# Moving the operand tile of the half-width products within SBUF, and leaving out their one split product

## The chip, the cores and the metric

The kernel runs on one core of a Trainium2 chip. The metric is the device time of one execution in microseconds; several executions are taken, and their median counts. Lower is better.

## The reference

One encoder layer over 512 positions of width 1024, everything in float32:

```python
x = x + 0.5 * swiglu(rms_norm(x, ffn1_norm), ffn1_w_gate, ffn1_w_up, ffn1_w_down)
h = rms_norm(x, mix_norm)
u = h @ w_in                      # [ fourier group 512 | q 8x64 | k 2x64 | v 2x64 ]
f_out = fourier_mixer(u[..., :o0], fnet_w, fnet_b)
a_out = gqa_attention(u[..., o0:o1], u[..., o1:o2], u[..., o2:], q_norm, k_norm)
x = x + jnp.concatenate([f_out, a_out], axis=-1) @ w_out
x = x + 0.5 * swiglu(rms_norm(x, ffn2_norm), ffn2_w_gate, ffn2_w_up, ffn2_w_down)
return rms_norm(x, final_norm)
```

`swiglu(h, wg, wu, wd)` is `(silu(h @ wg) * (h @ wu)) @ wd`, with a hidden width of 2752, that is 21 chunks of 128 and one of 64. The two feed-forward networks are where most of the work lies, and the change touches only them.

## The kernel before, in words

**Precision.** Each float32 operand is kept as a high part (rounded to the type that the listing calls float32r) and a low part (the rest). A product is then three matmuls: high weights by high data, high by low, low by high. In every matmul one operand is the stationary one (its weights, 128 by 128, loaded into TensorE ahead of the matmul by a load of its own) and the other is the moving one, which is streamed past it, 512 or 256 columns wide.

**Order.** TensorE's instructions and the DMA issues of SP are emitted in the written order (`in_order`). The other engines' orders are set by the framework's scheduler.

**A feed-forward network** (`ffn`) handles its 21 hidden chunks in four groups. The first chunks are computed plainly (`gate`: one product 512 columns wide for the gate and one for the up projection). For all others, each chunk's gate and up projections are computed together as a two-by-two block product with seven block products instead of eight (`operands` builds the seven combinations of the data once per network, `prepare` builds the combinations of the weights per chunk, `seven` multiplies). The two halves of the positions make the columns of such a block, so every one of these products is 256 columns wide. They are the half-width products of the title. They are issued in `multiply`, line 420: seven products per chunk, each with 4 row blocks and 3 matmuls, so 84 matmuls per chunk. There are six calls of `seven`, three in each network, one for each group but the first. After the half-width products of a group come the products of the down projection (`down`, issued at line 184, output tile `dn`), 512 columns wide. One last product of the group (step 9 of its last chunk, 12 matmuls) is put in between them, after the first row block of the down projection.

**Where the operands lie.** The SBUF address of an operand matters for the change, so here are the places, counted in 4-byte words within a partition. The tile `ring` holds the weights as stationary operands; its slots begin 16 words (`FRONT`) into the tile `whole`, and they lie a multiple of 64 words apart. All places below are given against these slots, modulo 64.

- The data of the first stage and of the down projection (`hh`, `hl`, `at`) begin 12 words before a slot (`NEAR`, `LOWER`). They are read as moving operands in a turned order: `turned` takes four words, steps on by 16 words, and comes back for the next four.
- `rt`, the tile of all operands of the half-width products, has the data's seven combinations, high and low. It is allocated behind `at`, and it begins 16 words before a slot. It is read straight, word after word.
- In the mixing stage, the Fourier group's projection (lines 1007 to 1009) also has products 256 columns wide, read straight, and none of them split: there the weights are the moving operand, 36 words after a slot (`FURTHER`), and the data `hh`, `hl` the stationary one, 12 words before a slot. So the moving operand lies 48 words after the stationary one, which is 16 before it modulo 64: the same distance as for `rt`.
- Where the last products of the kernel are 256 wide (lines 186 to 189, output tile `last`), the weights are pushed 4 words on (`SKIP`), so that the moving operand lies 16 words before them.

**Split products.** `parts_of(n)` gives the column ranges in which the product number `n` is issued. For `n == 1` (`CUT[0]`) it gives columns 0 to 64 and 64 to 256, so that this one matmul becomes two; for any other number it gives the whole 256. In `multiply` the number is drawn from `count`, which is made anew in each call of `seven` and begins at 0. So the second matmul of each call is split, and no other.

Of the kernel before, what the change touches and what calls it, by code (L numbers as in the profile page):

```python
# [7 lines left out]
F32R = mybir.dt.float32r  # L8
# [5 lines left out]
P = 128  # L14
S = 512
# [11 lines left out]
ROOM = 64  # L27
# [7 lines left out]
HALF = S // 2  # L35
USES = "a11", "a12", "s1", "s2", "s4", "s3", "a22"
PIECES = (0, 2, 2, 0, 2, 1, 1)
KH = KD // 2
# [48 lines left out]
def encoder(ctx, tc, A, out):  # L87
# [19 lines left out]
    def bank(name):  # L107
        return pp.tile([P, S], F32, tag="bank", name=name)
# [18 lines left out]
    def lows(lo, src, hi):  # L127
        nc.vector.tensor_tensor(out=lo, in0=src, in1=asf(hi), op=ALU.subtract)  # L128
# [31 lines left out]
    def parts_of(n):  # L160

        return (slice(0, CUT[1]), slice(CUT[1], HALF)) if n == CUT[0] else (slice(0, HALF),)
# [119 lines left out]
    def ffn(norm, after, wgu, wd, wdt, groups, opening, closing):  # L282
# [4 lines left out]
        n_ = norm.n  # L287
        n_plain = len(groups[0])
        with tc.tile_pool(name=f"act{n_}", bufs=1) as ap, tc.tile_pool(name=f"sums{n_}", bufs=2) as sp:
            room(ap, 128)  # L290
            acts = ap.tile([P, PLACES * 2 * S + ROOM], F32R, name=f"at{n_}")
            at = acts[:, FRONT + LOWER : FRONT + LOWER + PLACES * 2 * S].rearrange("p (n a b) -> p n a b", a=2, b=S)
            rt = ap.tile([P, 7, 2, KH, HALF], F32R, name=f"rt{n_}")
            wt, raws = [], {}
            free, where = list(range(PLACES)), {}

            def place(j):
                where[j] = free.pop(0)
                return where[j]
# [61 lines left out]
            def give(*ts):  # L361
                for t in ts:
                    taken[:] = [q for q in taken if q is not t]
                    (shared if any(t is q for q in slots[KD:]) else own).append(t)
# [42 lines left out]
            def seven(js, done):  # L407

                done = [done]
                banks = {}  # L410
                count = iter(range(84 * len(js)))

                def multiply(ps, wn, on, w, first):

                    (whi, wlo), (mhi, mlo) = w[wn], (part[on][:, i] for i in range(2))
                    for i in range(KH):
                        ks = slice(i * P, (i + 1) * P)
                        for o, (a, b) in enumerate(((whi, mhi), (whi, mlo), (wlo, mhi))):
                            for t in parts_of(next(count)):
                                nc.tensor.matmul(  # L420
                                    ps[:, t], a[:, ks], b[:, i, t], start=first and i == 0 and o == 0,
                                    stop=i == KH - 1 and o == 2, skip_group_check=not first,
                                )
                    give(*w.get((wn, "slots"), ()))

                def kept(ps, n, j):
                    t = sp.tile([P, HALF], F32, tag=n, name=f"{n}{n_}_{j}")
                    nc.scalar.copy(t, ps)  # L428
                    return t

                def step(j, w, n):
                    b = banks.setdefault(j, {})
                    if n == 0:
                        b["r"] = bank(f"r{n_}_{j}")[:, :HALF]
                        multiply(b["r"], "a11", "b11", w, True)
                        b["p1"] = kept(b["r"], "p1", j)
                    elif n == 1:
                        ps = bank(f"p2{n_}_{j}")[:, :HALF]
                        multiply(ps, "a12", "b21", w, True)
                        b["g"] = tp.tile([P, S], F32, tag="g", name=f"g{n_}_{j}")  # L440
                        nc.vector.tensor_tensor(out=b["g"][:, HALF:], in0=ps, in1=b["p1"], op=ALU.add)
                    elif n == 3:
                        b["q"] = bank(f"q{n_}_{j}")[:, :HALF]
                        multiply(b["q"], "s1", "t1", w, True)
                        b["p5"] = kept(b["q"], "p5", j)
                    elif n == 4:
                        multiply(b["r"], "s2", "t2", w, False)
                        b["u2"] = kept(b["r"], "u2", j)
                    elif n == 5:
                        multiply(b["q"], "s4", "b22", w, False)  # L450
                        nc.vector.tensor_tensor(out=b["g"][:, :HALF], in0=b["q"], in1=b["u2"], op=ALU.add)  # L451
                        nc.scalar.activation(b["g"], b["g"], AF.Silu)  # L452
                    elif n == 6:
                        multiply(b["r"], "s3", "t3", w, False)
                        b["u"] = tp.tile([P, S], F32, tag="u", name=f"u{n_}_{j}")
                        nc.scalar.copy(b["u"][:, :HALF], b["r"])
                        nc.vector.tensor_tensor(
                            out=b["u"][:, :HALF], in0=b["u"][:, :HALF], in1=b["p5"], op=ALU.add
                        )
                    elif n == 9:  # L460
                        multiply(b["r"], "a22", "t4", w, False)
                        u, i = b["u"], place(j)
                        h, l = at[:, i, 0], at[:, i, 1]
                        nc.scalar.copy(u[:, HALF:], b["r"])  # L464
                        nc.vector.tensor_tensor(out=u, in0=b["g"], in1=u, op=ALU.mult)  # L465
                        nc.scalar.copy(h, u)
                        lows(l, u, h)
                        del banks[j]

                for s in range(7 * len(js)):  # L470
                    i, n = divmod(s, 7)
                    if n == 2 and i:
                        step(js[i - 1], done[i - 1][0], 9)
                    if n == 0 and i + 1 < len(js):
                        done.append(prepare(js[i + 1]))
                        ahead = list(done[-1][1])
                    if n != 2:
                        step(js[i], done[i][0], n)
                    if i + 1 < len(js):
                        for _ in range(PIECES[n]):  # L480
                            f, *a = ahead.pop(0)
                            f(*a)
                return lambda: step(js[-1], done[-1][0], 9)
# [65 lines left out]
            for gi, group in enumerate(groups):  # L549
                last = gi == len(groups) - 1  # L550
                ahead = []
                if gi:
                    rest = seven(range(group[0] + 1, min(group[-1] + 2, NF)), ready)
                else:
                    lent = [acts[:, FRONT + i * KD * P : FRONT + (i + 1) * KD * P] for i in range(PLACES - 4, PLACES)]
                    plain.extend(lent)
                    row = []
                    pss = dict(enumerate(opening(gate, lambda: norm.column([norm.acc]), lambda: row.append(norm.row()))))
                    back(lent[:2])
                    due, parts, left = [*pss, "t"], list(range(KH)), range(2 * len(pss), 2 * n_plain)  # L560
                    pss["t"] = [gate(2 * NF)]
                    tail_weights()
                    for i, c in enumerate(left):
                        pss.setdefault(c // 2, []).append(gate(c, by_dma=i in (1,) if n_ else i > 0))
                        if due:
                            j = due.pop(0)
                            evacuate(at[:, place(j)], n_, pss[j], norm)
                        if c % 2 and c != left[-1]:
                            due.append(c // 2)
                        while len(parts) * len(left) > (len(left) - 1 - i) * KH:  # L570
                            o = parts.pop(0)
                            operands(row[0], o, o + 1)

                    def rest():
                        evacuate(at[:, place(n_plain - 1)], n_, pss[n_plain - 1], norm)
# [167 lines left out]
    with in_order():  # L743
        ffn(n0, n1, A["wgu1"], A["wd1"], A["wdt1"], GROUPS1, opening1, None)
# [3 lines left out]
    with tc.tile_pool(name="mix", bufs=1) as mp, tc.tile_pool(name="mixt", bufs=1) as mt:  # L748
# [384 lines left out]
        prob, parts, pts, outs, pair, zs, zps, sps, mxs = {}, {}, {}, {}, {}, {}, {}, {}, {}  # L1133
# [278 lines left out]
    with in_order():  # L1412
        ffn(n2, n3, A["wgu2"], A["wd2"], A["wdt2"], GROUPS2, lambda gate, column, row: [[gate(0, {KD - 1: column}), gate(1, {3: row})]], closing)
# [122 lines left out]
```

## Time and profile before

| what | value |
|---|---|
| times of three executions | 820.65, 821.0, 823.26 us |
| their median | 821.0 us |
| the profiled execution's own time | 820.94 us |
| the span of its instructions | 818.9 us |
| what lies around the span | 2.04 us |
| instructions of TensorE (matmul) | 5362 |

In the rows of the profile, PE stands for TensorE's matmuls and PEld for its loads of weights, DVE for VectorE, ACT for ScalarE, POOL for GpSimd. A row of a group gives the source line, the engine, the operation, what it writes and reads by the names in the program (`r<-rt,ring`), the stationary and the moving shape, the count, the busy time in us and the mean duration of one in ns. Matmuls are pipelined: one matmul lasts longer than the distance from it to the next. So a distance is read from the starts of a row of matmuls, or from the chain of work that ended last, where each entry is counted from the end of the one before.

### The profile page before, as it was taken

To read this page: it belongs to the slowest core of one execution; us is meant where nothing else is said; L and a number is where in the kernel's file an instruction comes from. 1 tells how busy PE (TensorE), PEld (TensorE's weight loads), DVE (VectorE), ACT (ScalarE), POOL (GpSimd) and SP (SyncE) were. 2 spreads that over 40 slices of the span, in tenths; PEclk is the share of its full clock that TensorE was granted. 3 is DMA by queue.
4 is the path that set the end of the run, shared out by engine and by line. 5 is a ranking of instruction groups with operands and counts; after the bars stand their busy time and mean duration, and the time that the engine had idled before them with its cause. 6 is when DMAs were issued, how large, how long until landed. Compare 5 with 4: busy or idle time off the path is not lost.

```text
span 818.9 us, 13611 instructions
## 1 busy us (share of the span) xinstructions
PE 812.4 (99%) x5362; PEld 746.1 (91%) x5362; DVE 637.5 (78%) x1003; ACT 483.1 (59%) x810; POOL 29.3 (4%) x31
## 2 busy tenths in 40 slices
PE   9999999999999999999999999999999999999997
PEld 7889999899989998889998888899989999899987
DVE  7898896479856847799998578999945896479574
ACT  7763674257523735699998448456632673257462
POOL 0110000000000000221000001100000000000001
PEclk9999999999999999999999999999999999999999
DMA  7664322333141223342101234542232322322222
GB/s 258 174 145 179 124 93 77 124 104 142 59 151 71 90 70 116 129 147 66 65 26 52 77 112 127 123 176 108 94 122 114 127 100 69 132 104 97 69 78 103
DMA packets 31568, 89.97 MB, mean 110 GB/s; under 512 B 3728, under 2 KB 9232, under 8 KB 31504
## 3 DMA queue, kind: packets, MB, share of 16 engines
q1 hardware_dynamic: 27776, 82.61, 29.1%
q0 software_dynamic: 3008, 5.51, 3.7%
q10 hardware_dynamic: 720, 0.98, 0.3%
q8 instruction: 42, 0.69, 0.3%
q14 instruction: 22, 0.18, 0.1%
HBM read 84.24 MB, written 2.10 MB: 105 GB/s over the span
## 4 chain that ended last, share of the span: by engine, by line
PE 95%; DVE 2%; ACT 1%; POOL 1%; issue 1%; DMA 0%; POOLq 0%; DVEq 0%; ACTq 0%
PE dn L184 25%; PE r L420 23%; PE q L420 12%; PE gu L184 8%; PE mix L184 6%; PE p L420 6%; PE gu L709 3%; PE mix L1203 2%; PE mix L1169 2%; PE mix L1007 1%; PE mix L1008 1%; PE mix L1009 1%; PE mix L1066 1%; PE mix L1143 1%; PE mix L1144 1%
## 5 line engine op out<-in xcount | busy, mean ns | idle before, releaser
L420 PE MATMUL r<-rt,ring 128*128 128x256 f32 x1686 | 209.2, 276 | 0.0
L184 PE MATMUL dn<-at,ring 128*128 128x512 f32 x900 | 202.5, 380 | 0.0
L420 PEld LDWEIGHTS r<-rt,ring 128*128 128x128 f32 x1686 | 200.3, 188 | 0.8
L184 PEld LDWEIGHTS dn<-at,ring 128*128 128x128 f32 x900 | 168.0, 188 | 28.3
L420 PE MATMUL q<-rt,ring 128*128 128x256 f32 x840 | 106.6, 276 | 0.0
L128 DVE TENSOR_TENSOR ring<-s,ring 128x1024 fp32r<-128x1024 f32 x70 | 85.5, 1221 | 23.8 <-ACT ring L379 20.8
L420 PEld LDWEIGHTS q<-rt,ring 128*128 128x128 f32 x840 | 100.4, 188 | 0.0
L544 DVE SCALAR_TENSOR_TENSOR gx<-dn,gx 128x512 f32<-128x512 f32 x61 | 41.9, 688 | 67.1 <-PE dn L184 67.1
L379 ACT CAST ring<-s 128x1024 fp32r<-128x1024 f32 x70 | 73.5, 1050 | 28.3 <-PE p L420 13.7
L170 ACT CAST ring<-raw_dn 128x768 fp32r<-128x768 f32 (+3 forms) x58 | 45.3, 784 | 72.8 <-PE dn L184 61.9
L128 DVE TENSOR_TENSOR ring<-raw_dn,ring 128x768 fp32r<-128x768 f32 (+3 forms) x58 | 51.5, 892 | 5.7 <-PE r L420 4.4
L420 PE MATMUL p<-rt,ring 128*128 128x256 f32 x420 | 53.3, 276 | 0.0
L128 DVE TENSOR_TENSOR ring<-raw_g,ring 128x1024 fp32r<-128x1024 f32 x35 | 42.7, 1220 | 11.7 <-PE p L420 10.2
L420 PEld LDWEIGHTS p<-rt,ring 128*128 128x128 f32 x420 | 50.2, 188 | 0.0
L184 PE MATMUL gu<-ring 128*128 128x512 f32 x216 | 48.9, 381 | 0.0
L379 ACT CAST ring<-raw_g 128x1024 fp32r<-128x1024 f32 x35 | 36.8, 1051 | 17.2 <-DMA raw_g<-in_wgu 11.5
L184 PEld LDWEIGHTS gu<-ring 128*128 128x128 f32 x216 | 40.4, 188 | 6.9
L428 ACT COPY p<-r 128x256 f32<-128x256 f32 x35 | 12.9, 369 | 44.9 <-PE r L420 44.6
L452 ACT ACTIVATE g<-g 128x512 f32<-128x512 f32 x35 | 22.2, 633 | 23.9 <-DVE g L451 23.6
L388 ACT CAST ring<-raw_u 128x512 fp32r<-128x512 f32 x35 | 21.8, 624 | 16.0 <-PE q L420 15.7
L184 PE MATMUL mix<-near,ring 128*128 128x512 f32 x120 | 28.8, 381 | 0.0
L465 DVE TENSOR_TENSOR u<-g,u 128x512 f32<-128x512 f32 x35 | 24.0, 687 | 6.1 <-ACT u L464 6.0
(266 smaller groups left out, 1314.3 us busy)
## 6 DMA issues: line engine op xcount, KB each, us to landing
raw_g<-in_wgu SPq DMA_DIRECT2D x35, 512.0 KB, 3.8
raw_u<-in_wgu SPq DMA_DIRECT2D x35, 512.0 KB, 4.3
raw_dn<-in_wd SPq DMA_DIRECT2D x40, 384.0 KB, 3.1
raw_gu<-in_wgu SPq DMA_DIRECT2D x12, 512.0 KB, 3.7
raw_o<-in_wo SPq DMA_DIRECT2D x8, 512.0 KB, 3.5
raw_dn<-in_wd SPq DMA_DIRECT2D x8, 448.0 KB, 3.7
raw_wq<-in_wins SPq DMA_DIRECT2D x4, 512.0 KB, 3.5
raw_f<-in_winf SPq DMA_DIRECT2D x4, 512.0 KB, 3.5
```

The source lines that it names most:

```text
L128: nc.vector.tensor_tensor(out=lo, in0=src, in1=asf(hi), op=ALU.subtract)
L170: nc.scalar.copy(hi[:, :n, :], raw[:, :n, :])
L184: nc.tensor.matmul(ps, a, b, start=first and b is mhi and a is whi, stop=last and a is wlo)
L379: nc.scalar.copy(hi, src)
L388: nc.scalar.copy(hi, src)
L420: nc.tensor.matmul(ps[:, t], a[:, ks], b[:, i, t], start=first and i == 0 and o == 0, stop=i == KH - 1 and o == 2, skip_group_check=not first,
L452: nc.scalar.activation(b["g"], b["g"], AF.Silu)
L465: nc.vector.tensor_tensor(out=u, in0=b["g"], in1=u, op=ALU.mult)
L544: nc.vector.scalar_tensor_tensor(out=x[d][:, t], in0=ps[:, t], scalar=0.5, in1=x[d][:, t], op0=ALU.mult, op1=ALU.add)
L709: nc.tensor.matmul(turned(pss[c]), w[:, k % 2, c], turned(m[k]), start=k == 0 and m is hh and w is hi, stop=k == KD - 1 and w is lo,)
L1169: nc.tensor.transpose(pts[n][:, c * P : (c + 1) * P], prob[t, b, c][:, kc * P : (kc + 1) * P], ident)
L1203: nc.tensor.matmul(turned(outs[t, b]), w, turned(p), start=kc == 0 and i == 0, stop=kc == 3 and i == 1)
```

## The change

The tile of all operands gets 64 words more than it needs, and the operands begin 52 words into it. Modulo 64 they then lie 36 words after a slot of the weights instead of 16 before. The pool's later tiles move by 64 words and so keep their places modulo 64. The counter begins at 2, so that no product of `multiply` has the number 1, and none is split.

```diff
@@ -290,7 +290,8 @@
             acts = ap.tile([P, PLACES * 2 * S + ROOM], F32R, name=f"at{n_}")
             at = acts[:, FRONT + LOWER : FRONT + LOWER + PLACES * 2 * S].rearrange("p (n a b) -> p n a b", a=2, b=S)
-            rt = ap.tile([P, 7, 2, KH, HALF], F32R, name=f"rt{n_}")
+            parts = ap.tile([P, 7 * S * KH + ROOM], F32R, name=f"rt{n_}")
+            rt = parts[:, 52 : 52 + 7 * S * KH].rearrange("p (n o k b) -> p n o k b", o=2, k=KH, b=HALF)
             wt, raws = [], {}
@@ -408,7 +409,7 @@
                 banks = {}
-                count = iter(range(84 * len(js)))
+                count = iter(range(2, 2 + 84 * len(js)))
 
                 def multiply(ps, wn, on, w, first):
```

## The prediction

> **What bounds the kernel now.** I read the head of the page first, then the chain of work that ended last.
>
> ```profile
> span 818.9 us, 13611 instructions
> PE 812.4 (99%) x5362; PEld 746.1 (91%) x5362; DVE 637.5 (78%) x1003; ACT 483.1 (59%) x810; POOL 29.3 (4%) x31
> PEclk9999999999999999999999999999999999999999
> PE 95%; DVE 2%; ACT 1%; POOL 1%; issue 1%; DMA 0%; POOLq 0%; DVEq 0%; ACTq 0%
> ```
>
> TensorE is busy for 99% of the span at the full granted clock, and 95% of the chain is its own work. A busy matmul is not a fast one, though, so the question is how far apart the matmuls start. The groups by form give the counts of the half-width products (line 420), and the table by stages, over the six stretches in which they run, says whether they wait.
>
> ```profile
> L420 PE MATMUL r<-rt,ring 128*128 128x256 f32 x1674 | 209.0, 276 | 0.0
> L420 PE MATMUL q<-rt,ring 128*128 128x256 f32 x840 | 106.6, 276 | 0.0
> L420 PE MATMUL p<-rt,ring 128*128 128x256 f32 x420 | 53.3, 276 | 0.0
> L420 PE MATMUL r<-rt,ring 128*128 128x192 f32 x6 | 2.0, 334 | 0.0
> L420 PE MATMUL r<-rt,ring 128*128 128x64 f32 x6 | 1.2, 192 | 0.0
> sum 325.30, PE 325.30 PEld 325.14 DVE 283.87 ACT 203.56 POOL 0.00; mean PE 54.22 PEld 54.19 DVE 47.31 ACT 33.93 POOL 0.00
> ```
>
> There are 1674 + 840 + 420 = 2934 whole products and six pairs of pieces. Both the matmuls and the loads of weights are busy all 325.3 us of these stretches, VectorE 283.9 and ScalarE 203.6, and no half-width product waits (the last column is 0.0). What sets the time here is the distance at which one product follows another, and nothing else. The chain gives that distance.
>
> ```profile
> 74.16 1.49 PE r L420 x13
> 75.65 1.36 PE p L420 x12
> ...
> 81.09 2.72 PE r L420 x24
> ...
> 130.05 3.96 PE dn L184 x18
> 134.01 1.37 PE r L420 x12
> ```
>
> 24 products take 2.72 us, 113.3 ns each, and so it goes on: 12 take 1.36 us. The 18 products 512 wide take 3.96 us, 220.0 ns each.
>
> **The change part by part.** *The split.* It is in the first row: the 13 matmuls that open a call of `seven` take 1.49 us. The cover for an unsplit opening is in the trace too. The 12 matmuls at 134.01 also follow the down projection, have the same shape, operands of the same two tiles at the same distance, and no split. They take 1.37 us. So without the split an opening costs 1.49 - 1.37 = 0.12 us less, and six calls give 6 x 0.12 = 0.72 us. All of it is on TensorE, which never waits here, so all of it is on the path. That holds if the streams fall into step at once, as at 134.01, which was measured with the operands at their old place. What a late fall into step costs is in the next part.
>
> *The place of the operands.* This changes no count and no size. It changes from which words the moving operand is read while the next weights are loaded. The price is per product, times 2940 products (all of line 420 after the change), so a nanosecond is worth 2.94 us. What the trace has on it are products 256 columns wide, read straight, elsewhere. First the Fourier projection, in the timeline of TensorE, whose first column is the start:
>
> ```profile
> 410.32 0.28 PE L1007 MATMUL mix<-ring 128*128 128x256 f32 x1
> ...
> 411.38 0.28 PE L1007 MATMUL mix<-ring 128*128 128x256 f32 x1
> ...
> 412.96 0.28 PE L1009 MATMUL mix<-ring 128*128 128x256 f32 x1
> 413.08 0.40 PE L186 MATMUL mix<-ring,chan 128*128 128x512 f32 x1
> ```
>
> These have the old distance of `rt` (48 words ahead, which is 16 behind modulo 64). The first nine starts, from 410.32 to 411.38, are 1.06 / 9 = 117.8 ns apart. The next fourteen, to 412.96, are 1.58 / 14 = 112.9 apart, which is the 113.3 of the half-width products within the rounding. So a stream of such products has a slow gait and a fast one; at this distance it finds the fast one, here after nine products, at 134.01 after one. The gait also shows in the duration: rows of the same lines, from windows before and after the fall into step.
>
> ```profile
> L1008 PE MATMUL mix<-ring 128*128 128x256 f32 x1 | 0.3, 281 | 0.0
> ...
> L1008 PE MATMUL mix<-ring 128*128 128x256 f32 x2 | 0.6, 275 | 0.0
> ```
>
> Now the last product of that stream, at 412.96. While it runs, the weights being loaded are those of the next line, `chan`, and they lie at the same place modulo 64 as the ring's slots. The moving operand is 36 words after a slot. That is exactly the pair of places that the change gives to all half-width products. Its group is the first row, and the chain's entries around it follow.
>
> ```profile
> L1009 PE MATMUL mix<-ring 128*128 128x256 f32 x1 | 0.3, 281 | 0.0
> ...
> 413.01 0.11 PE mix L1008
> 413.12 0.12 PE mix L1009
> ```
>
> It came out of a stream in the fast gait, and it alone lasts 281 again, with 0.12 us to itself instead of 0.11. Two other pairs of places point the same way: the position products (line 1066) are 256 wide, read straight, at distances other than -16.
>
> ```profile
> L1066 PE MATMUL mix<-pos,near 128*128 128x256 f32 x4 | 0.6, 281 | 0.0
> L188 PE MATMUL mix<-ring 128*128 128x256 f32 x1 | 0.3, 284 | 0.0
> ```
>
> All last 280 or more. Those streams are four to six products long, too short to tell whether they would have fallen into step later. That is the gap in the evidence: no row shows a long straight stream at the new distance. So I bound it. From above: 0.12 us, so 120 - 113.3 = 6.7 ns, 2940 x 6.7 = 19.7 us. From the other side: a stream may start tighter than 113.3 too. The tightest row of full matmuls with a load each are the transposes in the chain.
>
> ```profile
> 371.90 0.66 PE mix L1169 x6
> ```
>
> That is 110 ns each; 3.3 less, 2940 x 3.3 = 9.7 us gained. Between the ends I take the 117.8 of the slow gait, because the one product at the new distance has the duration of that gait (281): 2940 x (117.8 - 113.3) = 13.2 us lost.
>
> The page TensorE: Matmul & The Clock Gate of the Trainium skill (Part 2, step by step) says that TensorE has two independent read ports into SBUF, so that loading the next weights takes nothing from the running matmul. By that rule the place of the operand could not matter, and the sum would be the 0.72 us alone, 820.2; that is the first rival below. The trace does not bear it out in full: the same products of the mixing stage, same shape, same tiles, nothing waiting, have two durations (the timeline's row first, then its group, then that of the usual gait).
>
> ```profile
> 339.26 3.89 PE L184 MATMUL mix<-ring 128*128 128x512 f32 x16
> L184 PE MATMUL mix<-ring 128*128 128x512 f32 x16 | 3.9, 393 | 0.0
> L184 PE MATMUL dn<-at,ring 128*128 128x512 f32 x900 | 202.5, 380 | 0.0
> ```
>
> Here 16 products stay in a slow gait: (3.89 - 0.393) / 15 = 233.1 ns apart instead of 220.0. A slow gait can hold for a long stretch, then. It need not end by itself.
>
> *The rest.* The writes into `rt` (casts, subtractions, a few accumulating DMAs) are the same instructions at an address 208 bytes further. They run before the stretches, beside TensorE's plain products. Nothing is moved past a queue and no wait is added. When TensorE gets slower, ScalarE and VectorE get more cover, not less; nothing else is late next.
>
> **The sum.** It is made against the profiled execution's own 820.94 us (818.9 us of span and 2.04 around it; the median of the three executions is 821.0, so the same sum holds for it). 820.94 - 0.72 + 13.2 = 833.4 us.
>
> **The rivals.** *The streams fall into step all the same* (not slower). The mechanism is that of 134.01 and 410.32: each product is a little late until it no longer meets the load of weights, and then it stays there. It happens at the old distance, from every kind of start that the trace has, within nine products. If the new distance has such a step too, then the place costs at most 9 x 4.5 ns in each of the twelve stretches of half-width products, 0.5 us in all, and the split is saved: 820.94 - 0.72 = 820.2 us, with the late step 820.7. It decides from the point at which the extra distance of a product, 4.5 ns at first, dies away within some ten products. For it speaks that this step is robust where seen; against it, the product at 412.96, which lost its step at once when the distance became 36.
>
> *The slow gait is the deeper one* of 339.26, 13.1 ns per product: 2940 x 13.1 = 38.5 us, 858.7 us. Against it: no half-width product that follows another of its kind is that slow.
>
> *The products come closer than now*, down to the 110 ns of the transposes: 820.94 - 0.72 - 9.7 = 810.5 us. Against it: at the four places where 256-wide products run in step, none is under 113. By the formula of the same page (Back-to-back issue gap) 256 columns take 262 cycles, about 109 ns, and the sum would be about 808; the trace has 113.3 in nearly every row instead.
>
> *Some groups fall into step and others don't*, as with the two gaits of one shape in the mixing stage: anything between 820 and 833. I count it with the forecast where it costs over 0.3%.
>
> **How the numbers follow.** About 0.3%, 2.5 us, is what a measurement of this kernel can tell from no change. The slow gait of 4.5 to 6.7 ns per product, or part of the groups in it, gets 0.55; the deeper gait 0.05; the fall into step 0.3; the closer products 0.1. So faster 0.1, same 0.3, slower 0.6. The predicted time is that of the likeliest, 833.4 us; its own range goes from 826 (half the groups slow) to 842 (6.7 ns on all, 820.94 - 0.72 + 19.7 = 839.9, and the spread of a run). The range must also reach the fall into step, 820.2 with its spread, so it goes from 819.8 to 842. It leaves out the deeper gait, the closer products, and a little of the rest.
>
> **What would show it.** In the profile after, line 420 has 1680 products 256 wide for `r` and no piece of 64 or 192. If the forecast is right, their mean duration is 281 or more instead of 276 and a row of 12 in the chain takes 1.41 us or more instead of 1.36, while `dn` stays at 220.0. If the rows of 12 read 1.36 right from the opening, the first rival holds, and the mistake is to have read one product that lost its step as a gait that stays. If they read 1.49, it is the deeper gait; under 1.34, the closer products. If a row of 12 opens with 1.41 and goes on with 1.36, the step is found late. If `dn` or the mixing stage changes its distance, the cause lies in how a stretch begins and not in the new distance.

## The result, and the profile after

The changed kernel takes 836.0 us (median of four executions, 835.74 to 837.54), the kernel before 821.86 us in the same comparison (820.65 to 823.26). The ratio is 1.0175, with a 95% interval from 1.0152 to 1.0198: slower by 14 us. The profiled execution took 836.20 us, its span 834.1 us, so 15.3 us more than the profiled execution before. The forecast was 833.4 us. The ratios and intervals here and below leave out one execution, of the kernel without the split, which took 4677.07 us.

The head of the page after:

```profile
span 834.1 us, 13598 instructions
PE 826.2 (99%) x5356; PEld 760.3 (91%) x5356; DVE 640.3 (77%) x1003; ACT 484.6 (58%) x810; POOL 29.4 (4%) x31
PEclk9999999999999999999999999999999999999999
```

There are six matmuls less, which are the six second pieces, and TensorE is busy 13.8 us more. The clock is the same. VectorE, ScalarE and GpSimd do the same number of instructions in the same busy time, to within 3 us. The groups by form say where TensorE's time went (the half-width products have moved from line 420 to 421, since the change adds a line).

```profile
L421 PE MATMUL r<-rt,ring 128*128 128x256 f32 x1680 | 217.2, 280 | 0.0
L184 PE MATMUL dn<-at,ring 128*128 128x512 f32 x900 | 202.7, 380 | 0.0
L421 PE MATMUL q<-rt,ring 128*128 128x256 f32 x840 | 111.0, 280 | 0.0
L421 PE MATMUL p<-rt,ring 128*128 128x256 f32 x420 | 55.5, 280 | 0.0
```

The three groups of line 421 are busy 217.2 + 111.0 + 55.5 = 383.7 us. Before, the same groups had 209.0 + 106.6 + 53.3, and 2.0 + 1.2 in pieces, together 372.1. (Where two matmuls of different groups overlap, both groups count the time, and the two pieces of a split product overlap with its neighbours too, so the distances below are the better measure. In the kernel with the tile at its old place and no split, which comes below, the three groups are 208.5 + 106.6 + 53.3 = 368.4 us, 15.3 less than here.) The mean of `dn` has stayed at 380 ns. The chain gives the distances:

```profile
74.11 1.42 PE r L421 x12
75.52 1.43 PE p L421 x12
...
81.22 2.85 PE r L421 x24
84.07 1.42 PE p L421 x12
...
132.48 3.98 PE dn L184 x18
136.46 1.42 PE r L421 x12
137.88 4.19 PE dn L184 x19
```

An opening is now 12 products in 1.42 us, where it was 13 in 1.49. But every later row of 12 takes 1.42 or 1.43 where it took 1.36, and 24 take 2.85 where they took 2.72. From 74.11 to 84.07 there are seven rows of 12, 84 products in 9.96 us, 118.6 ns each instead of 113.3. The whole first stretch, 492 products from 74.11 to 132.48, gives the same 118.6. 2940 x 5.3 = 15.6 us lost, 0.7 us gained at the openings: 14.9 of the 15.3 us between the two profiled executions. The twelve products at 136.46, which took 1.37 us at the old place, take 1.42 as well. The view of the tile gives the shortest, the median and the longest duration of a group, here of the group `q`, first of the changed kernel and then of the kernel before:

```profile
L421 PE MATMUL q<-rt,ring x840: 277/280/283, 76.8 to 785.6; 128*128 128x256 f32 x168
```

```profile
L420 PE MATMUL q<-rt,ring x840: 276/276/276, 76.8 to 770.5; 128*128 128x256 f32 x168
```

Before, all 840 lasted 276 ns. After, none did. So the slow gait is not a late start that heals: no row of the chain and no product of this group comes into step.

### The profile page after: what moved, and what is told of

It reads as the page before. It is cut to its first block, busy times and chain, and to the rows that moved or that the text cites. A ratio compares the mean times of both kernels' runs of the same rounds, so it can differ in the third digit from the quotient of the medians.

```text
span 834.1 us, 13598 instructions
## 1 busy us (share of the span) xinstructions
PE 826.2 (99%) x5356; PEld 760.3 (91%) x5356; DVE 640.3 (77%) x1003; ACT 484.6 (58%) x810; POOL 29.4 (4%) x31
## 4 chain that ended last, share of the span: by engine, by line
PE 94%; DVE 2%; ACT 1%; issue 1%; POOL 1%; DMA 1%; POOLq 0%; DVEq 0%; ACTq 0%
PE dn L184 25%; PE r L421 24%; PE q L421 12%; PE gu L184 8%; PE mix L184 6%; PE p L421 6%; PE gu L710 3%; PE mix L1204 2%; PE mix L1170 2%; PE mix L1009 1%; PE mix L1008 1%; PE mix L1010 1%; PE mix L1067 1%; PE mix L1144 1%; PE mix L1145 1%
## 5 line engine op out<-in xcount | busy, mean ns | idle before, releaser
L421 PE MATMUL r<-rt,ring 128*128 128x256 f32 x1680 | 217.2, 280 | 0.0
L421 PEld LDWEIGHTS r<-rt,ring 128*128 128x128 f32 x1680 | 207.8, 188 | 0.8
L421 PE MATMUL q<-rt,ring 128*128 128x256 f32 x840 | 111.0, 280 | 0.0
L421 PEld LDWEIGHTS q<-rt,ring 128*128 128x128 f32 x840 | 104.5, 188 | 0.0
L421 PE MATMUL p<-rt,ring 128*128 128x256 f32 x420 | 55.5, 280 | 0.0
L421 PEld LDWEIGHTS p<-rt,ring 128*128 128x128 f32 x420 | 52.3, 188 | 0.0
L465 ACT COPY u<-r 128x256 f32<-128x256 f32 x35 | 13.1, 374 | 27.5 <-PE r L421 27.5
```

The costliest lines, as they stand in the source:

```text
L421: nc.tensor.matmul(ps[:, t], a[:, ks], b[:, i, t], start=first and i == 0 and o == 0, stop=i == KH - 1 and o == 2, skip_group_check=not first,
```

## The experiments

The theory: the distance between the moving operand and the slots of the weights, modulo 64 words, decides whether a stream of straight half-width products comes into step. The rivals: the split product had brought the streams into step, and leaving it out cost the time; or the new place is slow in itself, whatever the distance.

**The place alone.**

```diff
-            rt = ap.tile([P, 7, 2, KH, HALF], F32R, name=f"rt{n_}")
+            parts = ap.tile([P, 7 * S * KH + ROOM], F32R, name=f"rt{n_}")
+            rt = parts[:, 52 : 52 + 7 * S * KH].rearrange("p (n o k b) -> p n o k b", o=2, k=KH, b=HALF)
```

> The operand tile is moved by 52 words as in the change, and the split product is kept. Theory (the distance between the moving operand and the next weights sets the gait): the pieces can't bring the stream into the fast gait, products stay about 118.6 ns apart after every opening, and the time is that of the changed kernel or up to 1 us more, 836 to 837 us. Rival (the split is what brings the streams into step, and leaving it out is what cost 15 us): 12 products take 1.36 us again after the opening, and the time is that of the kernel before, 821 us.

Measured: 836.57 us, ratio to the kernel before 1.0189 (1.0174 to 1.0205). The chain:

```profile
74.49 1.53 PE r L421 x13
76.02 1.42 PE p L421 x12
77.44 1.43 PE q L421 x12
```

The opening with its split takes 1.53 us, and then the products go on in the slow gait. The split does not bring the step at this distance. The rival has fallen.

**The split alone.**

```diff
-                count = iter(range(84 * len(js)))
+                count = iter(range(2, 2 + 84 * len(js)))
```

> The operand tile stays where it was, and the split is left out. Theory: every opening falls into step at once, as the twelve products between the two parts of the down projection did before; an opening of 12 takes 1.37 us instead of 1.49 for 13, six times 0.12 us, so 0.7 us less than the kernel before (ratio 0.9991, just about what five rounds can show). Rival (the split brings the step): the streams stay in the slow gait, 836 us.

Measured: 820.12 us against 820.89, ratio 0.9990 (0.9979 to 1.0002). The times alone don't tell it from no change. The chain does:

```profile
73.90 1.37 PE r L420 x12
75.26 1.36 PE p L420 x12
```

The opening takes 1.37 us instead of 1.49 and is in step with the next row: 0.12 us less, and the span of the profiled execution is 818.0 instead of 818.9. So at the old place the split had only a cost.

**The place in the second network alone.**

```diff
-            rt = ap.tile([P, 7, 2, KH, HALF], F32R, name=f"rt{n_}")
+            parts = ap.tile([P, 7 * S * KH + ROOM], F32R, name=f"rt{n_}")
+            rt = parts[:, (52 if n_ else 0) : (52 if n_ else 0) + 7 * S * KH].rearrange("p (n o k b) -> p n o k b", o=2, k=KH, b=HALF)
-                count = iter(range(84 * len(js)))
+                count = iter(range(2, 2 + 84 * len(js)))
```

> No split; the tile is moved by 52 words in the second network only (1512 of the 2940 half-width products). Theory (a price per product, 5.3 ns): 1512 x 5.3 = 8.0 us more and 0.7 less than before, 828 us; 12 products take 1.36 us in the first network and 1.42 in the second. Rival (something that happens once, at an opening or in what a slow stretch leaves behind): either no change in the second network or one that isn't in proportion, under 824 or over 832 us.

Measured: 828.41 us, ratio 1.0096 (1.0082 to 1.0110). Rows of the chain in the first and in the second network:

```profile
74.04 1.37 PE r L421 x12
75.40 1.36 PE p L421 x12
...
537.69 1.42 PE r L421 x12
539.11 1.43 PE p L421 x12
```

Over the kernel without split and with the tile at its old place that is 828.41 - 820.12 = 8.3 us for 1512 products, 5.5 ns each, where the chain of the changed kernel gave 5.3. It is a price per product, and it does not reach into the other network.

**The distance restored at the new place.** Here the slots of the weights, the data `hh` and `hl`, and `at` are all moved, so that they keep their distances to one another; `rt` stays where the change put it, modulo 64, and is again 16 words before a slot.

```diff
-FRONT, LOWER, NEAR = 16, -12, 4
+FRONT, LOWER, NEAR = 68, -12, 4
-    whole = cp.tile([P, FRONT + NS * KD * P + 2 * ROOM], F32R, name="ring")
+    whole = cp.tile([P, 16 + NS * KD * P + 2 * ROOM + 32], F32R, name="ring")
-        [whole[:, k * KD * P + o * S + NEAR : k * KD * P + (o + 1) * S + NEAR] for k in range(KD)] for o in range(2)
+        [whole[:, k * KD * P + o * S + 52 + NEAR : k * KD * P + (o + 1) * S + 52 + NEAR] for k in range(KD)] for o in range(2)
-            at = acts[:, FRONT + LOWER : FRONT + LOWER + PLACES * 2 * S].rearrange("p (n a b) -> p n a b", a=2, b=S)
-            rt = ap.tile([P, 7, 2, KH, HALF], F32R, name=f"rt{n_}")
+            at = acts[:, 24 : 24 + PLACES * 2 * S].rearrange("p (n a b) -> p n a b", a=2, b=S)
+            parts = ap.tile([P, 7 * S * KH + ROOM], F32R, name=f"rt{n_}")
+            rt = parts[:, 20 : 20 + 7 * S * KH].rearrange("p (n o k b) -> p n o k b", o=2, k=KH, b=HALF)
-                count = iter(range(84 * len(js)))
+                count = iter(range(2, 2 + 84 * len(js)))
-                    lent = [acts[:, FRONT + i * KD * P : FRONT + (i + 1) * KD * P] for i in range(PLACES - 4, PLACES)]
+                    lent = [acts[:, 36 + i * KD * P : 36 + (i + 1) * KD * P] for i in range(PLACES - 4, PLACES)]
```

> The operand tile stays at its new place modulo 64 words, and the weights' slots (with the other operands that are read against them) are moved, so that the distance is again 16 words before a slot. No split. Theory (the distance counts, not the place): the half-width products are 113.3 ns apart, 12 in 1.36 us. Rival (the new place itself is slow, because the operand no longer begins at a multiple of 16 words): 118.6 ns, 12 in 1.42 us. The total is not compared, since the mixing stage's distances change with the slots: it is read from the stretches of the half-width products alone.

Measured: 821.9 us in a single execution, and in the chain:

```profile
74.49 1.39 PE r L421 x12
75.88 1.36 PE p L421 x12
...
81.32 2.72 PE r L421 x24
```

113.3 ns again. The distance counts and not the place. The opening takes 1.39 us, 0.03 more than in step, so the step is found some products later than at 73.90 above (1.37). That is how the Fourier projection began before the change: late, and then in step.

**Other distances.** Which others would do? The next runs have no split and one number changed, the words by which the tile's operands are moved. First 48 words, 32 after a slot:

```diff
-            rt = parts[:, 52 : 52 + 7 * S * KH].rearrange("p (n o k b) -> p n o k b", o=2, k=KH, b=HALF)
+            rt = parts[:, 48 : 48 + 7 * S * KH].rearrange("p (n o k b) -> p n o k b", o=2, k=KH, b=HALF)
```

> No split; the tile is moved by 48 words, so the operands lie 32 words after a slot of the weights. Theory (the distance counts in steps of 16 words: every multiple of 16 lets the stream fall into step, and 36 is slow because it is none): 12 products in 1.36 us, 820.2 us. Rival (the one distance of 16 words before a slot, modulo 64, is special): a slow gait, 12 products in 1.40 us or more, over 831 us.

Measured: 835.87 us.

```profile
73.67 1.43 PE r L421 x12
...
80.80 2.84 PE r L421 x24
```

Then 16 words, at the place of a slot:

```diff
+            rt = parts[:, 16 : 16 + 7 * S * KH].rearrange("p (n o k b) -> p n o k b", o=2, k=KH, b=HALF)
```

> No split; the tile is moved by 16 words, so the operands begin at the very place of a slot modulo 64. Theory (multiples of 16 words): the stream falls into step, 820.2 us. Rival (only 16 before a slot): a slow gait; the position of the short rows of the mixing stage at this distance, 280 and 284 ns long, is then that of the long streams too, some 118 to 120 ns apart, 833 to 840 us.

Measured: 840.46 us.

```profile
75.50 1.44 PE p L421 x12
...
81.26 2.88 PE r L421 x24
```

The first theory of which distances are good, the multiples of 16 words, has fallen with these two: 32 and 0 are slow. Then 4 words, 12 before a slot:

```diff
+            rt = parts[:, 4 : 4 + 7 * S * KH].rearrange("p (n o k b) -> p n o k b", o=2, k=KH, b=HALF)
```

> No split; the tile is moved by 4 words, so the operands lie 12 words before a slot, the distance at which the down projection's turned products run at their best. Theory (multiples of 16 words for a straight reading): a slow gait like that of 36, about 118.6 ns, 836 us. Rival (4 words are too little to matter, or what is good for the turned products is good for the straight ones): 113.3 ns, 820.2 us.

Measured: 837.54 us.

```profile
73.62 1.44 PE r L421 x12
...
80.78 2.86 PE r L421 x24
```

Four words, 16 bytes, from the old place cost as much as 52. The changed kernel with the turned order of reading:

```diff
-                                    ps[:, t], a[:, ks], b[:, i, t], start=first and i == 0 and o == 0,
+                                    turned(ps[:, t]), a[:, ks], turned(b[:, i, t]), start=first and i == 0 and o == 0,
```

> The changed kernel, 36 words after a slot and no split, but the half-width products read their moving operand, and write their output, in the turned order of the down projection. The result is the same. Theory (distance and order of reading go together, and 36 is the same modulo 16 as the 12 before a slot of the down projection): the stream falls into step, 113.3 ns, 820 us. Rival (36 is a bad distance for any order, or a half-width product is too short for the turned order): 118 ns or more, 836 us or over.

Measured: 834.1 us.

```profile
74.22 1.42 PE r L421 x12
75.64 1.43 PE p L421 x12
77.07 1.42 PE q L421 x12
...
79.89 1.41 PE q L421 x12
81.30 2.85 PE r L421 x24
```

Some rows are shorter by 0.01 us, and the time, of a single execution, is 1.9 us under that of the changed kernel; that is all. 36 is slow in this order too. The theory of this run has fallen as well. Four more distances, with the words 60, 32, 40 and 24 in the same line, in this order:

```diff
+            rt = parts[:, 60 : 60 + 7 * S * KH].rearrange("p (n o k b) -> p n o k b", o=2, k=KH, b=HALF)
+            rt = parts[:, 32 : 32 + 7 * S * KH].rearrange("p (n o k b) -> p n o k b", o=2, k=KH, b=HALF)
+            rt = parts[:, 40 : 40 + 7 * S * KH].rearrange("p (n o k b) -> p n o k b", o=2, k=KH, b=HALF)
+            rt = parts[:, 24 : 24 + 7 * S * KH].rearrange("p (n o k b) -> p n o k b", o=2, k=KH, b=HALF)
```

> No split; the tile is moved by 60 words, so the operands lie 20 words before a slot, 4 words from the old place on the other side. Theory now (one narrow good distance of 16 words before a slot, modulo 64, since 32, 0 and -12 all were slow): a slow gait, 117 to 120 ns, 832 to 841 us. Rival (the good distance is wide towards the other side): 113.3 ns, 820.2 us.

> No split; the tile is moved by 32 words, so the operands lie 16 words after a slot, half of 64 from the old place. Theory (modulo 64): a slow gait, 117 to 120 ns, 832 to 841 us. Rival (the pattern repeats after 32 words): 113.3 ns, 820.2 us.

> No split; the tile is moved by 40 words, so the operands lie 24 words after a slot. Theory (one good distance): a slow gait, 117 to 120 ns, 832 to 841 us. Rival (a second good distance lies between those tried): 113.3 ns, 820.2 us.

> No split; the tile is moved by 24 words, so the operands lie 8 words after a slot. Theory (one good distance): a slow gait, 117 to 120 ns, 832 to 841 us. Rival (a second good distance lies between those tried): 113.3 ns, 820.2 us.

Measured: 837.73, 833.0, 840.44 and 832.06 us. The chains, in the same order:

```profile
81.21 2.86 PE r L421 x24
```

```profile
81.07 2.83 PE r L421 x24
```

```profile
81.50 2.88 PE r L421 x24
```

```profile
75.94 1.40 PE r L421 x12
77.34 1.40 PE p L421 x12
...
82.94 2.80 PE r L421 x24
```

All four are slow; 8 words after a slot is the least so, with 116.7 ns a little under what was expected. Here are all nine distances, each without split; the time of 24 products is from the chain, the distance between two is that over 24. A step of 0.01 us in the second column is 0.4 ns in the third. The totals of -16 and 36 are medians, the others single executions; beside them the kernel before took 820.89 to 821.86 us, so the totals are compared to about 1 us.

| words after a slot, modulo 64 | 24 products, us | one product, ns | time, us |
|---|---|---|---|
| -16 | 2.72 | 113.3 | 820.12 |
| 8 | 2.80 | 116.7 | 832.06 |
| 16 | 2.83 | 117.9 | 833.0 |
| 32 | 2.84 | 118.3 | 835.87 |
| 36 (the change) | 2.85 | 118.8 | 836.0 |
| -12 | 2.86 | 119.2 | 837.54 |
| -20 | 2.86 | 119.2 | 837.73 |
| 0 | 2.88 | 120.0 | 840.46 |
| 24 | 2.88 | 120.0 | 840.44 |

Of the sixteen places in steps of four words nine were tried, and one is good. Its neighbours on both sides are among the slow ones. So it is a narrow place. Seven places were not tried, so a second good one is not excluded. The total at 8 holds about 2 us that do not belong to the place: in that execution the half-width products began at 75.94 instead of some 74. The version that comes out below both kernels is the kernel before without its split, 0.7 us below the kernel before, a difference that its profile shows and its times alone do not.

## Why the prediction was right

**The bound.** TensorE's own distance between products set the time and still does; no half-width product waits for another engine after the change either (the last column is 0.0). That held.

**The split.** Forecast 0.12 us for each opening, 0.72 in all, from the twelve unsplit products at 134.01. The run without the split shows the opening at 1.37 us, as those twelve. At the new place the split would have cost nearly the same, 1.53 - 1.42 = 0.11 us.

**The place.** Forecast 4.5 ns for each product, 13.2 us; measured 5.3 ns, 15.6 us. The mechanism, a gait that stays slow, was right, and the term was a little too small. It was taken from the first nine products of the Fourier projection on their way into step (117.8 ns), while the stream that never gets there runs at 118.6. That the two are so close is in part luck: the 117.8 was measured at the good distance, and the slow distances run from 116.7 to 120.0 among themselves. The range of the forecast, 819.8 to 842 us, held the first rival's 820.2 too, so that the time lies in it says little. What bears the mechanism out are the signs: rows of 12 in 1.42 us (1.41 or more was forecast), though with a mean duration of 280 ns, where 281 or more was forecast. The upper bound, 6.7 ns from the one product that had the new distance, was not reached at 36: products of 277 to 283 ns follow one another in the stream, and a single one doesn't give their mean. At the distances 0 and 24 the mean does reach it, with 120.0. The forecast also took from 16 products of the mixing stage, 233.1 ns apart, that a slow gait can hold, but the row of the usual gait beside them, `dn<-at,ring`, has other tiles. The comparison with the same tiles bears it out: five products `mix<-ring` of the same shape, from 337.24 of the kernel before, take 1.27 us, which at a last duration of 0.39 us puts them 220 ns apart.

**The first rival**, that the streams fall into step all the same, was given 0.3 and fell: the late step is real, as the opening of 1.39 us with the restored distance shows, but of the nine distances tried only the one good distance has it. What spoke for it was seen at that distance alone, since all long straight streams of the kernel before had it. By the rule of two independent read ports (the Trainium skill, TensorE: Matmul & The Clock Gate, Part 2, step by step) the time would have been 820.2. The traces disagree with what the forecast drew from it, that the place could not matter: there are 113.3 ns at one distance and 116.7 to 120.0 at eight others, and no half-width product waits.

**The other rivals.** The deeper gait of 13 ns did not come, nor products closer than 113.3; the 110 ns that stood for them came from transposes, which are 128 columns wide and not 256, so that row had little to say here. And no group fell into step while others didn't. The forecast wanted `dn` to stay at 220.0, or else the cause would lie in how a stretch begins. The 18 products of `dn` behind a slow stretch take 3.98 us instead of 3.96, but the 126 that follow the next twelve half-width products take 27.73 us, 220.1 ns each, as they did before (27.72). So `dn` falls back to its distance.

**What stays open.** The runs show that the distance of the moving operand to the slots of the weights decides, and that it is a price per product. That the two reads get in each other's way is the natural reading, but no run took the loads of weights away, so it is argued and not shown. VectorE and ScalarE also write into the weights' slots meanwhile. They are busy 275.9 and 199.8 of the 324.0 us of these stretches after the change, while the slow gait is the same from row to row, so their writes are an unlikely cause; no run tested it. Nor did a run move the tile by 64 words alone: that places count modulo 64 rests on the layout, in which the slots lie at different multiples of 64 words from the operands and all of them share one gait. And it is not known why 16 words before a slot is the good distance.

## What to carry to other kernels

When TensorE is busy all the time, read the distance between matmuls, and compare it with the same shape elsewhere in the kernel: 113 against 119 ns is 5% of a product's distance, here 2% of the whole time, and no wait in the profile shows it. Where moving operands and weights lie against one another in SBUF can be worth that much; it takes a scan of places, since four words decide, and the rule of multiples of 16 words did not hold here. A good place that was found for one stream goes with both of its operands: 36 words after a slot was good for the Fourier projection, whose stationary operand lay 12 words before one, and slow for the half-width products, whose stationary operand lies at the slot.

## What the runs showed that had not been expected

- The good place is less than 8 words wide: 12 and 20 words before a slot cost 5.9 ns a product (119.2 against 113.3), 16 before it nothing.
- The slow distances are not equally slow. They go from 116.7 ns (8 words after a slot) to 120.0 (at a slot, and 24 after), 3.4 to 6.7 ns over the step.
- A stretch in the slow gait leaves a trace in what follows it: the 18 products of the down projection behind it take 3.97 or 3.98 us instead of 3.96 (3.98 at 132.48 above).
